# Attention's value product in a two-layer encoder: the values become the stationary operand, two heads share the array

## The chip, the cores and the metric

The kernel runs on one core of a Trainium2 chip. A core has five engines that run their own instruction streams in order and wait for one another through semaphores: TensorE (PE in the profile; its weight loads are listed apart as PEld), VectorE (DVE), ScalarE (ACT), GpSimd (POOL) and SyncE (SP, which here only issues DMAs). The metric is the time of one execution on the device, in microseconds.

## The reference, cut to what matters

Two layers of a streaming encoder on 512 tokens of 1024 features. Each layer: half a SwiGLU block, a mixing block, half a SwiGLU block, a norm. The mixing block has two head groups side by side, attention with 8 heads and a convolution module, whose outputs are concatenated and projected:

```python
for l in range(DEPTH):
    x = x + 0.5 * swiglu(rms_norm(x, ...), ...)
    p = rms_norm(x, mix_norm[l]) @ w_in[l]
    attn = mla_group(p[..., :o_kv], ...)          # 8 heads, 64 value columns each
    conv = conv_group(p[..., o_cv:], ...)         # GLU, depthwise conv of 31 taps, LayerNorm, silu
    x = x + jnp.concatenate([attn, conv], -1) @ w_out[l]
    x = x + 0.5 * swiglu(rms_norm(x, ...), ...)
    x = rms_norm(x, post_norm[l])
```

Inside attention each block of 128 queries sees the keys up to its own end (with a mask inside the last block):

```python
scores = einsum('bhqd,bhkd->bhqk', qs, ks).astype(float32) * scale
probs  = softmax(where(allowed, scores, -1e30))
out    = einsum('bhqk,bhkd->bqhd', probs, vs)
```

All arithmetic is float32 in the reference.

## The kernel before, in words

The residual x is held with features on the 128 partitions and the 512 tokens along the free dimension. The big products use three matmuls of split operands (`mm3`, L154 to L156, a rounded high part and a low remainder); attention itself uses plain float32 matmuls.

The mixing block (`mix_body`) first makes the projections, the queries `q`, the keys `kn` and the values `vs` (four tiles of 128 tokens by 8 x 64 columns, L900). Then attention runs head by head through five stages, written as a software pipeline: `ORDER = "t0s1p3v4o5"` names a stage and its lag in steps, and the loop at the end of attention emits in every step each stage for the head that is due.

- `turn` (L811, L816): transposes of queries and keys on TensorE, copied out by ScalarE (L813) and VectorE (L818).
- `scores` (L834, L835): for query block i a matmul over the (i+1) x 128 visible keys, the mask added by a second matmul; VectorE takes the row maximum (L836, result `mx`), ScalarE the exponential (L840), which also leaves the row's sum in `sums`. The score of block 1 (128x256) shares a bank with that of block 0 and comes last.
- `turn_p` (L855): ten transposes of the 128 x 128 blocks of probabilities, keys on the partitions afterwards; three evictions (L858), two by VectorE and one by ScalarE. Key block j keeps the query blocks j to 3 side by side, 512, 384, 256 and 128 columns.
- `values` (L868): for every query block t and key block j up to t one matmul with the turned probabilities stationary (128 columns) and the head's 64 value columns moving: ten a head. Two heads share a bank `po`. After the odd head VectorE takes 1/sum (L873, 8 numbers a partition) and multiplies it in (L875), so that the result has queries on the partitions and 2 x 64 value columns for each block.
- `turn_out` (L886): four transposes bring that to features on partitions, and `split` (L161 by ScalarE, L162 by VectorE) makes the high and low parts which the output projection reads as `at`.

Beside attention the convolution's taps run: channel groups 0 and 3 on VectorE (L922, one operation a tap, accumulated in PSUM, then copied out by ScalarE, L932), groups 1 and 2 as a product on ScalarE (L926, tile `pr` with three buffers) and an add on GpSimd (L930). Then GpSimd adds the four groups (L944 to L946) and TensorE forms the mean over channels with a matmul against `onesm` (L948). From it follow the LayerNorm, silu and the conv half of the projection's operand (L954 to L966, `cv`); meanwhile TensorE multiplies the attention half for the first output tiles (`early_groups`, L154 to L156).

```python
for c, kind in enumerate("DAAD"):        # cut: D on VectorE, A on ScalarE and GpSimd
    ...
G.tensor_tensor(ysum, ys[0], ys[1], ALU.add)
G.tensor_tensor(ysum, ysum, ys[2], ALU.add)
(G if YP else V).tensor_tensor(ysum, ysum, ys[3], ALU.add)
pm = bank()
T.matmul(pm, onesm, ysum, start=True, stop=True)
```

The order of the instructions on each engine is not that of the source. A planner (`schedule_with_timeline_sim=True`) chooses it from its own costs when the program is built, within the data's dependences and a few `issue_after` bounds. Tiles come from rotating pools: `tmps` (five buffers of 128 x 512), `small`, `ring` (35 buffers), and seven PSUM banks. A tile waits until the one that had its buffer before is no longer read.

Of the kernel before, what the change touches and what calls it, by code (L numbers as in the profile page):

```python
# [7 lines left out]
FP = mybir.dt.float32  # L8
# [4 lines left out]
ALU = mybir.AluOpType  # L13
AX = mybir.AxisListType

P = 128
# [4 lines left out]
NT = S // P  # L21
# [4 lines left out]
DV = 64  # L26
# [48 lines left out]
def encoder_kernel(ctx: ExitStack, tc: tile.TileContext, xT, consts, vecs, rgain, wgu1, wd1, wdq1,  # L75
# [7 lines left out]
    small = ctx.enter_context(tc.tile_pool(name="small", bufs=2))  # L83
# [3 lines left out]
    def nm(s):  # L87
        uid[0] += 1
        return f"{s}{uid[0]}"
# [4 lines left out]
    def tmp(w=S, dt=FP):  # L94
        return tmps.tile([P, w], dt, tag="t", name=nm("t"))

    def bank():
        return psum.tile([P, S], FP, tag="ps", name=nm("ps"))
# [4 lines left out]
    V, A, G, T = nc.vector, nc.scalar, nc.gpsimd, nc.tensor  # L103
# [8 lines left out]
    ident = cst[:, CID:CID + P]  # L112
# [46 lines left out]
    def split(src, made=slot):  # L159
        hi, lo = made(FR), made(FR)  # L160
        order["high"] = A.copy(hi, src).ins  # L161
        order["evicted"] = V.tensor_tensor(lo, src, hi.bitcast(FP), ALU.subtract).ins  # L162
        return hi, lo
# [46 lines left out]
    def spread(r):  # L210

        dg = tmp()
        V.tensor_tensor(dg.rearrange("p (t j) -> p t j", t=NT),
                        ident[:, None, :].to_broadcast([P, NT, P]),
                        r[:, :, None].to_broadcast([P, NT, P]), ALU.mult)
        ps = bank()
        order["spread"] = T.matmul(ps, ones, dg, start=True, stop=True).ins
        return ps
# [398 lines left out]
    def mix_body(kpool, l, gx, norm, done):  # L617
# [28 lines left out]
        cqT, ckT, pq, scqs, vs = [], [], [], [], []  # L646
# [114 lines left out]
        def up_kv(w, t, n=S):  # L761

            ts_ = slice(t * P, (t + 1) * P)
            ps = bank()
            for k in range(2):
                cs = slice(k * n, (k + 1) * n)
                mm3(ps, ckT[k][0][:, ts_], ckT[k][1][:, ts_], w[0][:, cs], w[1][:, cs], k == 0, k == 1)
            return ps
# [33 lines left out]
        at = []  # L802
# [3 lines left out]
        heads = [{} for _ in range(H)]  # L806
# [54 lines left out]
        def values(h):  # L861

            if h % 2 == 0:
                heads[h]["po"] = bank()
            po = heads[h - h % 2]["po"].rearrange("p (t h d) -> p t h d", t=NT, h=2)
            for t in range(NT):
                for j in range(t + 1):
                    T.matmul(po[:, t, h % 2], heads[h]["pt"][j][:, (t - j) * P:(t - j + 1) * P],  # L868
                             vs[j][:, h * DV:(h + 1) * DV], start=j == 0, stop=j == t)
            if h % 2 == 0:  # L870
                return
            rs = small.tile([P, NT, 2], FP, tag="rs", name=nm("rs"))
            V.reciprocal(rs, heads[h - 1]["sums"])  # L873
            o = tmp()
            V.tensor_tensor(o.rearrange("p (t h d) -> p t h d", t=NT, h=2), po,  # L875
                            rs[:, :, :, None].to_broadcast([P, NT, 2, DV]), ALU.mult)
            heads[h]["o"] = o

        def turn_out(h):

            if h % 2 == 0:
                return
            o = heads[h]["o"]
            ps = bank()
            for t in range(NT):
                T.transpose(ps[:, t * P:(t + 1) * P], o[:, t * P:(t + 1) * P], ident)  # L886
            at.append(split(ps, kept if len(at) < 2 else slot))

        STAGES = [({"t": turn, "s": scores, "p": turn_p, "v": values, "o": turn_out}[c], int(d)) for c, d in zip(ORDER[::2], ORDER[1::2])]

        wv = load_w(wkv[l, 1], WC, "uk")
# [4 lines left out]
        with tc.issue_after(order["turned"]):  # L896
            for t in range(NT):
                ps = up_kv(wv, t)
# [5 lines left out]
        for step in range(H + 6):  # L904
            for stage, lag in STAGES:
                h = step - lag
# [7 lines left out]
        for c in range(4):  # L914
# [4 lines left out]
            for k in range(CK - 2, -1, -1):  # L919
# [4 lines left out]
                pr = kpool.tile([P, S], FP, tag="pr", name=nm("pr"), bufs=3)  # L924
# [31 lines left out]
        r = st.token(CW)  # L956
        early_groups(range(E2, E3))
        pr = spread(r)
# [282 lines left out]
```

## Time and profile before

| | us |
|---|---|
| median of 3 runs | 1804.17 (1803.3 to 1804.97) |
| the profiled execution | 1804.94 |
| its span, first to last instruction | 1803.1 |
| PE busy | 1781.6 |
| DVE busy | 1493.0 |
| ACT busy | 1091.9 |
| POOL busy | 420.2 |
| mean granted TensorE clock | 0.998 |

A timeline row gives the start and the time it took in microseconds, engine, line, operation, output<-inputs with shapes and a count; in brackets stands how long the engine sat idle before it and what ended that. Rows that merge several instructions (x4) give the time from the first start to the last end. A table of windows gives, for each stretch, its length and the busy time and number of instructions of PE, PEld, DVE, ACT and POOL, then the granted TensorE clock, the DMA share and GB/s. A group row gives the busy time in all, the mean ns of one, and the idle time before. TensorE's matmuls overlap, so the cost of one in a row of many is the distance between starts, not its own duration. A float32 matmul shows as two records, a transpose as one.

### The profile page before, as it was taken

Reading aid. Unit: us, or ns where it says so; the run is one execution under the profiler, and the core shown is the slowest. Engines: PE = TensorE matmul, PEld = TensorE weight load, DVE = VectorE, ACT = ScalarE, POOL = GpSimd, SP = SyncE. Lnnn points to the kernel's source line nnn. Section 1 sums busy time; section 2 is a strip of 40 time slices with the busy share of each in tenths; the row PEclk is TensorE's granted clock in tenths of the full one; section 3 lists DMA queues with packets and bytes.
Section 4 is the critical chain, followed back from the end, with each engine's and each line's share of the span. In section 5 each row is a group of like instructions: output and inputs, shape, how many; then the busy total and the mean of one; then the engine's idle time right before and its main releaser. Section 6 shows DMA issues by size and latency. Waiting matters only on the chain. (4 is left out here: it accounts for less than half of the span.)

```text
span 1803.1 us, 29267 instructions
## 1 busy us (share of the span) xinstructions
PE 1781.6 (99%) x11334; PEld 1603.1 (89%) x11334; DVE 1493.0 (83%) x2263; ACT 1091.9 (61%) x1721; POOL 420.2 (23%) x343
## 2 busy tenths in 40 slices
PE   9999999999999999999999999999999999999998
PEld 7899999888788899999888999998978788999997
DVE  7898988689956989898779989876998668989884
ACT  5565656457953575756645656554779435656564
POOL 1000010258943000000310000002689410000102
PEclk9999999999999999999999999999999999999999
DMA  5657574325103466665426575743250125575742
GB/s 167 173 127 182 134 174 125 108 88 136 29 24 100 124 167 160 153 159 129 125 63 169 126 191 122 193 110 111 80 151 3 42 83 161 139 183 134 180 119 74
DMA packets 70412, 226.16 MB, mean 125 GB/s; under 512 B 7936, under 2 KB 8320, under 8 KB 70272
## 3 DMA queue, kind: packets, MB, share of 16 engines
q1 hardware_dynamic: 54000, 169.74, 29.7%
q0 software_dynamic: 16128, 54.53, 17.6%
q8 instruction: 89, 1.46, 0.3%
q14 instruction: 51, 0.42, 0.1%
q10 hardware_dynamic: 144, 0.00, 0.0%
HBM read 222.15 MB, written 2.10 MB: 124 GB/s over the span
## 5 line engine op out<-in xcount | busy, mean ns | idle before, releaser
L155 PE MATMUL ps<-r,wh 128*128 128x256 f32 (+1 forms) x2540 | 805.8, 318 | 0.0
L154 PE MATMUL ps<-r,wh 128*128 128x256 f32 (+1 forms) x2540 | 802.9, 320 | 2.3 <-ACT wh L1060 1.5
L156 PE MATMUL ps<-r,wl 128*128 128x256 f32 (+1 forms) x2348 | 750.0, 321 | 1.7 <-DVE wl L246 1.6
L154 PEld LDWEIGHTS ps<-r,wh 128*128 128x128 f32 x2540 | 480.4, 189 | 44.1 <-ACT wh L138 3.7
L155 PEld LDWEIGHTS ps<-r,wh 128*128 128x128 f32 x2540 | 481.4, 190 | 34.2 <-issue 1.4
L156 PEld LDWEIGHTS ps<-r,wl 128*128 128x128 f32 x2348 | 445.0, 190 | 36.7 <-DVE wl L246 3.2
L373 PE MATMUL ps<-xj,wh 128*128 128x512 f32 x864 | 304.8, 392 | 4.6 <-DVE t L426 4.6
L138 ACT CAST wh<-raw 128x1024 fp32r<-128x1024 f32 (+3 forms) x148 | 132.3, 903 | 203.6 <-PE ps L155 100.3
L390 POOL DMA_DIRECT2D ls<-in_wgu x72 | 62.5, 869 | 734.4 <-ACT ls L389 656.5
L244 ACT CAST wh<-fr 128x1024 fp32r<-128x1024 f32 (+1 forms) x160 | 157.8, 986 | 109.7 <-DVE fr L410 51.3
L144 DVE TENSOR_TENSOR wl<-raw,wh 128x1024 fp32r<-128x1024 f32 (+3 forms) x132 | 145.2, 1108 | 84.7 <-ACT wh L138 84.3
L246 DVE TENSOR_TENSOR wl<-fr,wh 128x1024 fp32r<-128x1024 f32 (+1 forms) x160 | 182.1, 1138 | 20.5 <-ACT wh L244 20.5
L373 PEld LDWEIGHTS ps<-xj,wh 128*128 128x128 f32 x864 | 161.3, 188 | 36.3 <-DVE t L426 6.2
L930 POOL TENSOR_TENSOR y<-y,pr 128x511 f32<-128x511 f32 (+14 forms) x120 | 158.1, 1318 | 54.9 <-ACT pr L926 47.5
L374 PE MATMUL ps<-xj,ls 128*128 128x256 f32 x576 | 161.3, 280 | 0.0
L246 DVE TENSOR_TENSOR wl<-raw,wh 128x1024 fp32r<-128x1024 f32 (+1 forms) x100 | 113.4, 1134 | 14.8 <-ACT wh L244 14.4
L244 ACT CAST wh<-raw 128x1024 fp32r<-128x1024 f32 (+1 forms) x100 | 98.1, 981 | 44.7 <-PE ps L155 27.7
L191 POOL TENSOR_TENSOR r<-r,t 128x512 f32<-128x512 f32 x45 | 75.1, 1678 | 175.7 <-ACT t L187 174.9
L374 PEld LDWEIGHTS ps<-xj,ls 128*128 128x128 f32 x576 | 108.3, 188 | 0.2
L389 ACT ACTIVATE ls<-fr 128x1024 fp32r<-128x1024 f32 (+1 forms) x56 | 56.1, 1001 | 85.3 <-PE ps L374 49.5
L926 ACT ACTIVATE pr<-m,vec 128x511 f32<-128x511 f32 (+14 forms) x120 | 85.8, 737 | 12.4 <-POOL y L930 12.4
L922 DVE SCALAR_TENSOR_TENSOR cv<-m,vec,cv 128x511 f32<-128x511 f32 (+14 forms) x120 | 87.8, 732 | 3.6 <-ACT cv L918 2.2
(242 smaller groups left out, 2926.2 us busy)
## 6 DMA issues: line engine op xcount, KB each, us to landing
fr<-in_wgu SPq DMA_DIRECT2D x112, 512.0 KB, 4.2
ls<-in_wgu POOLq DMA_DIRECT2D x72, 512.0 KB, 6.6
raw<-in_wgu SPq DMA_DIRECT2D x62, 512.0 KB, 4.9
fr<-in_wdq SPq DMA_DIRECT2D x48, 384.0 KB, 5.3
ls<-in_wdq POOLq DMA_DIRECT2D x32, 384.0 KB, 4.7
raw<-in_wd SPq DMA_DIRECT2D x32, 384.0 KB, 3.1
raw<-in_wd SPq DMA_DIRECT2D x32, 256.0 KB, 2.7
raw<-in_wcv SPq DMA_DIRECT2D x16, 512.0 KB, 3.6
```

The lines of the kernel that those rows point to most:

```text
L138: order["cast"] = A.copy(hi[:, :w], raw[:, :w]).ins
L144: (G if kind in POOLW.split() else V).tensor_tensor(lo[:, :w], raw[:, :w], hi[:, :w].bitcast(FP), ALU.subtract)
L154: T.matmul(o, lh, rh, start=first, stop=False, skip_group_check=free)
L155: T.matmul(o, lh, rl, start=False, stop=False, skip_group_check=free)
L156: order["mm"] = T.matmul(o, ll, rh, start=False, stop=last, skip_group_check=free).ins
L244: A.copy(hi[:, :w], src[:, :w])
L246: order["lo"] = V.tensor_tensor(lo[:, :w], src[:, :w], hi[:, :w].bitcast(FP), ALU.subtract).ins
L373: T.matmul(o, w[0][:, c], both, start=start and k == 0, stop=False, skip_group_check=True)
L374: last = T.matmul(o[:, 0:HS], w[1][:, c], both[:, 0:HS], start=False, stop=k == 3, skip_group_check=True).ins
L922: V.scalar_tensor_tensor(acc[:, s:], u[c][:, :S - s], tap(k), acc[:, s:], ALU.mult, ALU.add)
L926: A.activation(pr[:, s:], u[c][:, :S - s], AF.Copy, scale=tap(k))
L930: order["conv"] = G.tensor_tensor(acc[:, s:], acc[:, s:], pr[:, s:], ALU.add).ins
```

## The change

The product of probabilities and values is turned round. The values are now stationary (128 keys by 64 columns) and the turned probabilities move, key block by key block, over all query blocks that see them: four matmuls a head with 512, 384, 256 and 128 columns instead of ten with 64. The result has value columns on the partitions and queries along the free dimension: the even head of a pair is written to partitions 0 to 63 of the bank, the odd head to 64 to 127, so each matmul uses one half of the array's columns. Both heads are done when the odd head is due.

As the result no longer needs turning, `turn_out` only splits it. The reciprocal of the sums has queries on the partitions and must be turned instead: VectorE writes it 64 times over, 2 x 64 columns for each of the four query blocks (128 x 512 in all), TensorE turns four blocks, ScalarE copies them out of PSUM, and VectorE multiplies. Lines from L900 on stand one lower in the changed file; the text keeps the numbers of before for what both have, and the new lines are L866 (reciprocal), L870 (its turns), L872 (copy), L876 (matmuls) and L879 (product).

```diff
         def values(h):
             if h % 2 == 0:
-                heads[h]["po"] = bank()
-            po = heads[h - h % 2]["po"].rearrange("p (t h d) -> p t h d", t=NT, h=2)
+                return
+            rs = tmp()
+            V.reciprocal(rs.rearrange("p (t h d) -> p t h d", t=NT, h=2),
+                         heads[h - 1]["sums"][:, :, :, None].to_broadcast([P, NT, 2, DV]))
+            pr = bank()
             for t in range(NT):
-                for j in range(t + 1):
-                    T.matmul(po[:, t, h % 2], heads[h]["pt"][j][:, (t - j) * P:(t - j + 1) * P],
-                             vs[j][:, h * DV:(h + 1) * DV], start=j == 0, stop=j == t)
+                T.transpose(pr[:, t * P:(t + 1) * P], rs[:, t * P:(t + 1) * P], ident)
+            r = tmp()
+            A.copy(r, pr)
+            po = bank()
+            for j in range(NT):
+                for i in range(2):
+                    T.matmul(po[i * DV:(i + 1) * DV, j * P:], vs[j][:, (h - 1 + i) * DV:(h + i) * DV],
+                             heads[h - 1 + i]["pt"][j], start=j == 0, stop=j == NT - 1)
+            o = tmp()
+            V.tensor_tensor(o, po, r, ALU.mult)
+            heads[h]["o"] = o
+
+        def turn_out(h):
             if h % 2 == 0:
                 return
-            rs = small.tile([P, NT, 2], FP, tag="rs", name=nm("rs"))
-            V.reciprocal(rs, heads[h - 1]["sums"])
-            o = tmp()
-            V.tensor_tensor(o.rearrange("p (t h d) -> p t h d", t=NT, h=2), po,
-                            rs[:, :, :, None].to_broadcast([P, NT, 2, DV]), ALU.mult)
-            heads[h]["o"] = o
-
-        def turn_out(h):
-            if h % 2 == 0:
-                return
-            o = heads[h]["o"]
-            ps = bank()
-            for t in range(NT):
-                T.transpose(ps[:, t * P:(t + 1) * P], o[:, t * P:(t + 1) * P], ident)
-            at.append(split(ps, kept if len(at) < 2 else slot))
+            at.append(split(heads[h]["o"], kept if len(at) < 2 else slot))
```

## The prediction

> **What bounds the kernel now.** I read the page's busy line, then a table of windows around the only code that changes (attention, once per layer), then the timeline of that stretch engine by engine.
>
> ```profile
> span 1803.1 us, 29267 instructions
> PE 1781.6 (99%) x11334; PEld 1603.1 (89%) x11334; DVE 1493.0 (83%) x2263; ACT 1091.9 (61%) x1721; POOL 420.2 (23%) x343
> ```
> ```profile
> core 0: us, PE busy (x) PEld busy (x) DVE busy (x) ACT busy (x) POOL busy (x), PEclk, DMA share, GB/s
> 451.00:508.50 57.50, 55.06 (x402) 44.97 (x401) 50.05 (x97) 50.54 (x122) 52.09 (x43) 1.00 0.11 23
> 1344.00:1400.00 56.00, 53.79 (x393) 43.92 (x391) 49.16 (x96) 50.17 (x122) 51.48 (x43) 1.00 0.10 20
> ```
> TensorE looks like the bound overall, but in attention four engines are each within 13% of full: 57.5 us hold 55.1 of PE and 50 to 52 of the other three. What any of them is given there has little room. How the stretch ends:
>
> ```profile
> 493.36 0.72 DVE L922 SCALAR_TENSOR_TENSOR cv<-m,vec,cv 128x483 f32<-128x483 f32 x1
> 493.98 1.15 DVE L836 TENSOR_REDUCE mx<-ps 128x1 f32<-128x384 f32 x2
> 495.05 0.72 DVE L922 SCALAR_TENSOR_TENSOR cv<-m,vec,cv 128x482 f32<-128x482 f32 x1
> 497.59 0.60 ACT L932 COPY m<-cv 128x512 f32<-128x512 f32 x1
> ...
> 463.28 3.96 POOL L930 TENSOR_TENSOR y<-y,pr 128x511 f32<-128x511 f32 x3 [0.61 <-ACT pr L926]
> 467.90 3.95 POOL L930 TENSOR_TENSOR y<-y,pr 128x508 f32<-128x508 f32 x3 [0.67 <-ACT pr L926]
> 472.23 31.42 POOL L930 TENSOR_TENSOR y<-y,pr 128x505 f32<-128x505 f32 x24 [0.37 <-ACT pr L926]
> 503.60 1.27 POOL L944 TENSOR_TENSOR t<-m,y 128x512 f32<-128x512 f32 x1
> ...
> 506.29 1.26 POOL L946 TENSOR_TENSOR t<-t,m 128x512 f32<-128x512 f32 x1
> 507.24 0.69 DVE L875 TENSOR_TENSOR t<-ps,rs 128x512 f32<-128x512 f32 x1 [0.87 <-PE ps L868]
> 507.99 0.66 PE L886 MATMUL ps<-cst,t 128*128 128x128 f32 x4 [0.79 <-DVE t L875]
> 508.48 1.02 PE L948 MATMUL ps<-t,onesm 128*128 128x512 f32 x2
> ...
> 522.52 1.19 PE L154 MATMUL ps<-r,wh 128*128 128x512 f32 x4
> ```
> L948 (the mean over the conv channels) needs POOL's sum L944 to L946, whose last addend is VectorE's conv channel (tap 128x482, then the copy L932). In layer 0 that sum ends at 507.55, the attention tail at 508.4: both arrive together. From L948 a chain leads to 522.52, where the output projection first reads the conv half. So the price of this change is how far L948's start moves, per layer. The second layer has the same shape 892 us later, with one difference:
>
> ```profile
> 1387.06 0.71 DVE L922 SCALAR_TENSOR_TENSOR cv<-m,vec,cv 128x482 f32<-128x482 f32 x1
> 1400.97 2.08 PE L948 MATMUL ps<-t,onesm 128*128 128x512 f32 x2 [0.31 <-POOL t L946]
> 1416.68 1.21 PE L154 MATMUL ps<-r,wh 128*128 128x512 f32 x4
> ```
> ```profile
> 506.77:510.18 3.41, 2.63 (x14) 1.88 (x14) 1.57 (x3) 1.48 (x2) 0.79 (x1) 1.00 0.00 0
> 1397.64:1401.05 3.41, 2.31 (x20) 1.94 (x18) 1.38 (x2) 0.38 (x2) 3.12 (x3) 0.98 0.00 0
> 1401.05:1404.47 3.41, 3.41 (x7) 2.06 (x8) 2.07 (x4) 2.37 (x5) 0.00 (x0) 0.52 0.00 0
> ```
> After 3.41 us in which PE was busy 68%, the granted clock was 0.52 for the next 3.41; after one of 77% it stayed 1.00. L948 to L154 takes 14.04 us in layer 0 and 15.71 in layer 1, so one slow window costs 1.67.
>
> **The change, part by part (layer 0's clock).**
>
> *Matmuls.* Start to start:
>
> ```profile
> 468.27 2.44 PE L868 MATMUL ps<-m,r 128*128 128x64 f32 x20
> 470.55 0.65 PE L834 MATMUL ps<-r,r 96*128 96x256 f32 x2
> ...
> 460.47 1.12 PE L834 MATMUL ps<-r,r 96*128 96x512 f32 x2
> 461.43 0.19 PE L835 MATMUL ps<-mneg,mrow 128*128 128x64 bf16 x1
> ...
> 464.62 0.39 PE L834 MATMUL ps<-r,r 96*128 96x128 f32 x2
> 464.85 0.19 PE L835 MATMUL ps<-mneg,mrow 128*128 128x64 bf16 x1
> 464.88 0.91 PE L834 MATMUL ps<-r,r 96*128 96x384 f32 x2
> 465.62 0.19 PE L835 MATMUL ps<-mneg,mrow 128*128 128x64 bf16 x1
> ...
> 467.14 1.29 PE L855 MATMUL ps<-cst,r 128*128 128x128 f32 x10
> ```
> Removed: 2.28 a head, 4.56 a pair. Added: two heads times moving widths 512, 384, 256, 128; L834 gives 0.96, 0.74, about 0.48 and 0.23, so 2.4 a head: 4.8 a pair one after the other, 2.4 if the halves run together. Before shows no matmul on half the columns; bounds are thus -2.2 and +0.2 a pair, and I take the gain. It matters little, since PE will wait (below). The Trainium skill (TensorEngine Tiling, "Key Properties") says two things that pull apart: tiles run in parallel, and changing the tiling mode drains TensorE, which the changed program does ten times a layer; no row here shows either.
>
> *Turns.* Four L886 turns a pair become four of the reciprocals (new L870): same shape, 0.66 in the row above, no difference; the split reads SBUF instead of PSUM, none either. ScalarE gains a 128x512 copy a pair (L872), 0.61 by the ACT row below, 2.5 a layer: it has 7 us free, so nothing; uncovered, 2.5. Each pair now takes three `tmps` buffers of five instead of one, and the rotation gives POOL's first sum (L944) the buffer of pair 2's turned reciprocals: it has to wait for pair 2's product on VectorE, 506 to 508 in the walk below, where it ran at 503.6. Two adds later, at 509 to 511, POOL is still ahead of the last addend, so this costs nothing here. No DMA moves; SP's and POOL's order is unchanged.
>
> *The reciprocal.* This is the step that decides. L873 took the reciprocal of 8 numbers a partition; the new L866 takes the same 8 broadcast to 512 columns, four times a layer.
>
> ```profile
> L873 DVE RECIPROCAL rs<-sums x8: 187/193/197, 465.0 to 1392.6; 128x8 f32<-128x8 f32 x8
> ```
> ```profile
> L858 DVE COPY r<-ps 128x512 f32<-128x512 f32 x8 | 5.5, 684 | 0.4 <-PE ps L855 0.4
> L858 ACT COPY r<-ps 128x512 f32<-128x512 f32 x8 | 4.9, 614 | 0.8 <-PE ps L855 0.8
> L858 DVE COPY r<-ps 128x256 f32<-128x256 f32 x8 | 3.3, 415 | 0.4 <-PE ps L855 0.4
> ```
> ```profile
> L120 DVE MEMSET minus_half<- 128x8 f32 x1 | 0.1, 65 | 0.0
> ```
> COPY, the other one-input operation, has two sizes: (684-415)/256 = 1.05 ns a column, fixed part 146 ns. Eight columns at that rate would take 154, the reciprocal takes 193. With COPY's fixed part it costs (193-146)/8 = 5.9 ns a column, and 512 columns 3.15 us. Lower bound: any 128x512 operation's 0.69. Upper: MEMSET's fixed part (65-8 = 57), 17 ns a column, 8.8 us. I take 3.15, nearest in kind.
>
> VectorE's lane up to tap 482: 50.05 of work less the last L875 (0.69), plus 4 x (3.15-0.19) = 11.8, makes 61.2: from 451, 512.2 with no idle at all. The changed program's order gives the same from the other end. Head 7's three reductions, at 495.1 before, now come after three reciprocals (+8.9) and ahead of six taps (-3.7; a tap is 0.62 from start to start): near 500. Behind them stand pair 1's split, five evictions, the last reduction and five taps (505.4), pair 2's product (TensorE has it at 505 to 507), the last reciprocal (509 to 511), head 7's evictions, pair 2's split and two taps: 511.9 to 513.9. Then L932's copy (0.60), POOL's last add (1.26) and hand-overs (0.2): L948 starts at 514 to 516 instead of 508.48, +5.5 to +7.5; I take 6.3. Head 7's weights wait for the same evictions, so pair 3's product ends near 512 to 514.5, beside POOL's sum. Layer 1 the same (tap 482 to L948 is 13.9 us there, 13.4 here): 12.6 together.
>
> *Clock.* From 496 to 514 PE has the last score, head 6's and 7's turns, two of reciprocals and two products, some 8 us or 45%, under the 68% that slowed it: layer 0 now pays 1.67 after L948; layer 1 already did.
>
> Sum: 12.6 + 1.7 = 14.3. The profiled execution took 1804.94 (span 1803.1 plus 1.8 around) and becomes 1819.2; the median of the runs is 0.8 lower, so **1818.5**.
>
> **Rivals.**
>
> *The reciprocal has a shorter fixed part than COPY.* At 126 ns, between MEMSET's and COPY's, it costs 8.4 ns a column and 4.4 us: the lane ends at 517.2, L948 at 519.3, +10.8 a layer, 1804.2 + 21.6 + 1.7 = 1827.5. For it: nothing in the rows fixes that part. The Trainium skill (VectorE: DVE Perf Modes, "First, the fixed hardware budget") tells of an iterative divide with a repeat count of 8, by which 512 columns would take 8 x 512 = 4096 cycles; 193 ns for 8 columns is compatible with this if the rest is 126 ns.
>
> *The reciprocal is as cheap as its neighbours (0.69), still slower.* ScalarE then sets the tail. In the changed order all conv products L926 stand ahead of head 7's exponentials, and they have three buffers which POOL frees.
>
> ```profile
> 493.32 0.70 ACT L926 ACTIVATE pr<-m,vec 128x487 f32<-128x487 f32 x1 [0.60 <-POOL y L930]
> ...
> 494.37 0.36 ACT L840 ACTIVATE r<-ps,mx 128x128 f32<-128x128 f32 x1
> ```
> The last product can start three adds (31.42/24 = 1.31 each) before POOL's last add ends: 503.6 - 0.4 - 3.9 = 499.3; head 7's exponentials follow at 500.1, not 494.37. PE's rest from there (last score 0.5, half of head 6's turns and all of head 7's 1.8, two of the reciprocals' 0.9, two products of 2.4 to 4.8, 1.5 for copies between) takes 9.5 to 14: L948 at 509.6 to 514, +1.1 to +5.6; POOL's sum, behind pair 2's product at 505.6 to 508, comes at 509.7 to 512. With 2.6 a layer and the slow window: 1811.
>
> *Faster.* PE ran almost alone from 498 to 508; two pairs' products at half price leave it 4 us less, and pair 3 needs no turn behind its product. L948 is then held by POOL's sum, 507.55 less the waits POOL had (0.61, 0.67, 0.37), at best 505.9. A gain of at most 2.6 a layer, and 1.7 if layer 1 loses its slow window: 1797. It needs a reciprocal under 1.7 us (four of them must add less than the 6.0 us between the lane and L948), halves running together, and head 7 not held by ScalarE. The 0.193 row speaks against the first, the order against the last.
>
> *No change.* The same with PE's gain only filling waits: 1804, within 0.2% (3.6 us, about what a measurement of this kernel can tell from no change).
>
> **Chances.** Reciprocal near 3.15 us, 1818.5 (own range 1811 to 1824): 0.50. The 4.4 us one, 1827.5: 0.22. The cheap one with ScalarE's tail, 1811: 0.16, of which 0.04 lies within 0.2%. No change: 0.06. Faster: 0.06. So faster 0.06, same 0.10, slower 0.84. Below 1806 lie the faster case, no change and the best of the cheap one (0.14), above 1832 the dear end of the reciprocal's bounds (0.06): the range is 1806 to 1832.
>
> **What would show it.** RECIPROCAL 128x512 near 3.2 us, 0.7 or 4.4; VectorE busy without a gap up to tap 482, near 512 to 514; L948 starting at 514 to 516 and waiting for POOL, and POOL's last add for L932; PE with idle gaps from 496 on, and a clock near 0.5 around L948 in layer 0; new matmul pairs starting together or 0.48 apart per pass. The prediction is wrong if the reciprocal is cheap, if the scores that wait behind it starve ScalarE and so POOL much earlier (then more is lost), or if slow-clock windows spread over the whole stage.

## The result and the profile after

The changed kernel took 1830.63 us (median of 4 runs, 1828.4 to 1832.44) against 1803.74 (1802.81 to 1804.97) for the kernel before on the same chip: a ratio of 1.0148, 95% interval 1.0131 to 1.0166. The sign and the range held; the forecast of 1818.5 was 12.1 us too low.

The busy line of the page after:

```profile
span 1828.9 us, 28902 instructions
PE 1791.6 (98%) x11142; PEld 1585.7 (87%) x11142; DVE 1519.3 (83%) x2263; ACT 1099.6 (60%) x1729; POOL 422.3 (23%) x343
```

VectorE has 26.3 us more to do over the span (1519.3 against 1493.0), which is 8 x (3.34 - 0.19) = 25.2 for the reciprocals and little else; the span grew by 25.8. The summary of the new reciprocal's line (fastest, median and slowest in ns, then the first and the last start):

```profile
L866 DVE RECIPROCAL t<-sums x8: 3342/3342/3344, 465.4 to 1418.6; 128x512 f32<-128x512 f32 x8
```

The timeline of the changed kernel at the end of attention in layer 0 and at the same place in layer 1 (L921, L931, L943 to L945 and L947 are the lines that were L922, L932, L944 to L946 and L948):

```profile
517.63 0.98 PE L870 MATMUL ps<-cst,t 128*128 128x128 f32 x4 [3.42 <-DVE t L866]
518.54 3.66 PE L876 MATMUL ps<-r,m 128*64 128x512 f32 x16
...
519.49 0.72 DVE L921 SCALAR_TENSOR_TENSOR cv<-m,vec,cv 128x482 f32<-128x482 f32 x1
520.24 0.59 ACT L931 COPY m<-cv 128x512 f32<-128x512 f32 x1 [0.96 <-DVE cv L921]
520.97 1.27 POOL L945 TENSOR_TENSOR t<-t,m 128x512 f32<-128x512 f32 x1 [4.07 <-ACT m L931]
522.30 1.12 PE L947 MATMUL ps<-t,onesm 128*128 128x512 f32 x2
522.32 0.69 DVE L879 TENSOR_TENSOR t<-ps,t 128x512 f32<-128x512 f32 x1 [2.11 <-PE ps L876]
...
536.73 1.20 PE L154 MATMUL ps<-r,wh 128*128 128x512 f32 x4
...
1426.78 1.12 PE L947 MATMUL ps<-t,onesm 128*128 128x512 f32 x2
...
1441.31 1.21 PE L154 MATMUL ps<-r,wh 128*128 128x512 f32 x4
```

The chain is the predicted one: the last tap, ScalarE's copy, GpSimd's last add (which waited 4.07 us for it), the mean matmul. TensorE's own lane arrives with it: the last pair's products (518.54, 3.66 us long) end at 522.20. But the tap starts at 519.49 instead of 512, and the mean matmul at 522.30 instead of 508.48: 13.8 us in layer 0 (0.37 of it from ahead of attention). In layer 1 it starts 25.8 us later than before; 14.2 of these are layer 0's shift of the first conv product (536.73 against 522.52), and 1.8 arose between there and layer 1's first scores (1359.39 against 1343.43), so 9.8 are attention's own in layer 1. The work from the mean matmul to the conv product took 14.43 and 14.53, against 14.04 and 15.71.

Windows of the changed kernel show what VectorE did up to the end of that tap, and then the stretches of the clock:

```profile
451.00:520.21 69.21, 58.68 (x295) 36.20 (x295) 62.90 (x97) 53.71 (x126) 51.99 (x42) 0.86 0.10 20
...
472.90:479.75 6.85, 6.83 (x24) 4.65 (x24) 5.30 (x10) 4.81 (x12) 6.46 (x6) 0.53 0.01 2
...
490.00:496.80 6.80, 6.18 (x21) 3.85 (x20) 5.54 (x12) 6.58 (x17) 6.41 (x6) 0.53 0.00 0
...
507.05:510.50 3.45, 3.40 (x13) 1.46 (x13) 3.45 (x8) 2.34 (x7) 0.00 (x0) 0.57 0.00 0
...
517.30:520.70 3.40, 3.07 (x10) 1.38 (x12) 2.91 (x6) 1.04 (x2) 0.00 (x0) 0.57 0.01 2
```

VectorE's lane is 62.9 us of work (0.4 of it because the stage starts later) and 6.3 of idle time; 61.2 and none were predicted. Before, it had 0.89 of idle time up to the same tap:

```profile
451.00:495.77 44.77, 43.11 (x296) 33.31 (x295) 43.88 (x86) 43.75 (x108) 40.93 (x34) 1.00 0.14 28
```

TensorE's clock fell to about half four times inside attention, some 20 us in all; before it never did there. Each of the four windows follows 3.4 us in which TensorE was busy for only 1.88, 2.13, 1.78 and 0.30 us, or 55, 63, 52 and 9%, below the 68% that the prediction's rows show ahead of a slow window. The waits of VectorE (DVE) in this stretch (us in total, times, longest), and the rows of the three in the first line:

```profile
DVE mx L836 <- PE ps L835: 2.5, 3, 1.3
DVE t L879 <- ACT pr L925: 1.7, 2, 1.3
DVE mx L836 <- ACT t L872: 1.1, 1, 1.1
...
475.15 0.56 DVE L836 TENSOR_REDUCE mx<-ps 128x1 f32<-128x384 f32 x1 [0.51 <-PE ps L835]
477.07 0.69 DVE L836 TENSOR_REDUCE mx<-ps 128x1 f32<-128x512 f32 x1 [0.71 <-PE ps L835]
495.23 0.69 DVE L836 TENSOR_REDUCE mx<-ps 128x1 f32<-128x512 f32 x1 [1.26 <-PE ps L835]
```

The second and third row name ScalarE as what came last; the work VectorE reads there (`mx` from scores, `t` from products) comes from TensorE. So it waits for TensorE's scores and products, while TensorE in its turn waits for the reciprocal (3.42 us in the row of L870 above). The slow clock stands between the two: all three waits of the first row fall in the first two slow windows, in which TensorE was busy for 6.83 of 6.85 and 6.18 of 6.80 us, and the wait of 1.1 us ends at 480.77, just behind the first.

### The profile page after: what moved, and what is told of

It is laid out like the page before. It is cut to its first block, busy times and chain, and to the rows that moved or that the text cites. A ratio compares the mean times of both kernels' runs of the same rounds, so it can differ in the third digit from the quotient of the medians.

```text
span 1828.9 us, 28902 instructions
## 1 busy us (share of the span) xinstructions
PE 1791.6 (98%) x11142; PEld 1585.7 (87%) x11142; DVE 1519.3 (83%) x2263; ACT 1099.6 (60%) x1729; POOL 422.3 (23%) x343
## 5 line engine op out<-in xcount | busy, mean ns | idle before, releaser
L921 DVE SCALAR_TENSOR_TENSOR cv<-m,vec,cv 128x511 f32<-128x511 f32 (+14 forms) x120 | 87.6, 730 | 3.8 <-ACT cv L917 2.2
```

The costliest lines, as they stand in the source:

```text
L921: V.scalar_tensor_tensor(acc[:, s:], u[c][:, :S - s], tap(k), acc[:, s:], ALU.mult, ALU.add)
```

## The experiments

Four explanations of the doubled shift were to be told apart: the sum of VectorE's work; the 3.3 us for which one instruction blocks its lane; the slow clock of a TensorE that has less to do; and something in the other parts of the change. Each ratio is to the kernel before on the same chip, with its 95% interval. Attention itself starts up to 1 us earlier or 1.5 later from run to run (GpSimd's add of 128x511, at 463.28 before, shows by how much); where it matters, the shift is given.

**The reciprocal of 8 numbers, and a copy that spreads it** (of the changed kernel):

```diff
-            rs = tmp()
-            V.reciprocal(rs..., sums[..., None].to_broadcast([P, NT, 2, DV]))
+            sm = small.tile([P, NT, 2], FP, tag="rs", name=nm("rs"))
+            V.reciprocal(sm, heads[h - 1]["sums"])
+            rs = tmp()
+            V.tensor_copy(rs..., sm[:, :, :, None].to_broadcast([P, NT, 2, DV]))
```

> The changed kernel, but the reciprocal is taken of the 8 sums (0.19 us) and a plain copy writes it 64 times over (128x512, 0.69): 2.46 us less on VectorE, four times a layer, 9.8 a layer. Theory 1, the long reciprocal in VectorE's in-order lane is the whole cause: the mean matmul comes back from 522 to 509 to 511 in layer 0, and the time to 1804 to 1811. Theory 2, the emptier TensorE falls into slow-clock windows of its own accord and these hold the stage: at least three windows near 0.5 stay in layer 0's attention, and of the 26 us only about 12 come back: 1815 to 1822.

1814.69 us, ratio 1.005 (1.0035 to 1.0065). 15.9 of the 26.9 us came back, and the mean matmul starts at 511.31, of whose 2.83 us of shift 1.28 come from ahead of the stage: in layer 0 attention is only 1.55 us longer than before. The time lies between the forecasts, so the long reciprocal is not the whole cause, but theory 2's slow windows are absent: the mean clock of attention is 0.98, and VectorE is full up to its last tap.

```profile
451.00:501.87 50.87, 45.85 (x281) 29.82 (x279) 50.79 (x96) 50.66 (x123) 45.79 (x37) 1.00 0.15 32
...
451.00:523.00 72.00, 61.88 (x357) 41.62 (x356) 61.84 (x113) 58.30 (x135) 55.82 (x44) 0.98 0.10 23
...
511.31 1.13 PE L948 MATMUL ps<-t,onesm 128*128 128x512 f32 x2 [3.89 <-POOL t L946]
```

TensorE has the same matmuls as in the changed kernel, yet keeps its clock: without the long reciprocal the slow windows of this stage are gone. What is still lost lies behind the mean matmul of layer 0 (15.69 us to the conv product, with a slow window, against 14.04) and in layer 1, whose attention is 4.0 us longer than before.

**No wide operation on VectorE for it at all:**

```diff
-            V.reciprocal(rs..., ...)        # cut: the long one goes, and its buffer with it
+            V.reciprocal(sm, heads[h - 1]["sums"])
             for t in range(NT):
-                T.transpose(pr[:, t * P:(t + 1) * P], rs[:, t * P:(t + 1) * P], ident)
+                for i in range(2):
+                    T.matmul(pr[i * DV:(i + 1) * DV, t * P:(t + 1) * P],
+                             sm[:, t, i:i + 1].to_broadcast([P, DV]), ident, start=True, stop=True)
```

> The changed kernel, but nothing 128x512 wide is left to VectorE for the reciprocal: 8 numbers (0.19), and the turn is a product of the 64-fold repeated column of weights with the identity, eight of 64x128 a pair instead of four turns. VectorE has 12.6 us less a layer than in the changed kernel, TensorE some 1 to 1.3 more. Theory 1: the mean matmul at 506 to 510, 1799 to 1806. Theory 2: slow windows stay, some 1812 to 1820.

1812.81 us, ratio 1.0041 (1.0027 to 1.0054). Theory 1's 1799 to 1806 fails: with the reciprocal as cheap as before the change, the rest of it still loses 8.5 us. Now the mean matmul waits for GpSimd (POOL); a slow window follows that wait.

```profile
507.09 0.86 DVE L162 TENSOR_TENSOR r<-t,r 128x512 fp32r<-128x512 f32 x1 [0.69 <-ACT r L161]
...
507.48 1.59 POOL L944 TENSOR_TENSOR t<-t,y 128x512 f32<-128x512 f32 x1
509.14 1.26 POOL L945 TENSOR_TENSOR t<-t,m 128x512 f32<-128x512 f32 x1
...
510.46 2.08 PE L947 MATMUL ps<-t,onesm 128*128 128x512 f32 x2 [4.87 <-POOL t L945]
...
507.00:510.40 3.40, 0.00 (x0) 0.00 (x0) 0.86 (x1) 1.34 (x2) 3.24 (x3) 0.79 0.00 0
510.50:517.30 6.80, 6.80 (x17) 4.72 (x18) 4.47 (x7) 2.60 (x5) 0.00 (x0) 0.61 0.00 0
```

An add that took 1.26 on GpSimd took 1.59 beside the split L162, which in the changed kernel reads two operands from SBUF. The cost shows on both sides (line summary: fastest, median and slowest in ns, and group rows of the adds, before and then here):

```profile
L162 DVE TENSOR_TENSOR r<-ps,r x2: 692/692/692, 505.7 to 509.3; 128x512 fp32r<-128x512 f32 x2
...
L930 POOL TENSOR_TENSOR y<-y,pr 128x487 f32<-128x487 f32 (+29 forms) x36 | 44.8, 1244 | 4.2 <-ACT pr L926 1.6
```
```profile
L162 DVE TENSOR_TENSOR r<-t,r x2: 859/1120/1382, 503.7 to 507.1; 128x512 fp32r<-128x512 f32 x2
...
L929 POOL TENSOR_TENSOR y<-y,pr 128x487 f32<-128x487 f32 (+29 forms) x36 | 46.0, 1279 | 5.0 <-ACT pr L925 2.6
```

**The kernel before with the long reciprocal alone:**

```diff
-            rs = small.tile([P, NT, 2], FP, tag="rs", name=nm("rs"))
-            V.reciprocal(rs, heads[h - 1]["sums"])
+            rs = tmp()
+            rs4 = rs.rearrange("p (t h d) -> p t h d", t=NT, h=2)
+            V.reciprocal(rs4, heads[h - 1]["sums"][:, :, :, None].to_broadcast([P, NT, 2, DV]))
             ...                             # cut: the product reads rs4 as it is
```

> The kernel before with one edit: its reciprocal (8 numbers) is taken 64 times over, 128x512, as in the changed kernel; the old products, turns and splits stay. VectorE has 12.6 us more a layer. Theory 1: the mean matmul moves by 10 to 14 a layer, as in the changed kernel, and the time is 1824 to 1832. Theory 2: TensorE has 2.2 us a pair more to do than in the changed kernel, slow windows are fewer, and the lane alone decides: the mean matmul moves by 5 to 8, 1814 to 1820.

1833.75 us, ratio 1.0158 (1.0142 to 1.0173): theory 1. This one edit costs as much as the whole change (the intervals overlap). It has the old products and turns, so neither the halves of the array nor TensorE's saved work is needed for the loss. 25.2 us of added VectorE work cost about 29. Here it is the attention tail behind the last reciprocal, not the tap, that ends last. Up to the end of the last product VectorE idled 4.5 us, and the clock of that stretch was 0.95, where it was 0.86 in the changed kernel:

```profile
512.50 3.34 DVE L874 RECIPROCAL t<-sums 128x512 f32<-128x512 f32 x1
...
518.93 0.69 DVE L876 TENSOR_TENSOR t<-ps,t 128x512 f32<-128x512 f32 x1 [1.62 <-PE ps L868]
...
520.59 1.92 PE L949 MATMUL ps<-t,onesm 128*128 128x512 f32 x2
...
451.00:519.62 68.62, 60.76 (x404) 48.46 (x402) 64.13 (x99) 53.19 (x125) 52.84 (x43) 0.95 0.11 23
```

**The pair's products twice** (of the changed kernel):

```diff
+            for again in range(2):
                 for j in range(NT):
                     for i in range(2):
                         T.matmul(po[...], vs[j][...], heads[h - 1 + i]["pt"][j], ...)
```

> The changed kernel, but each pair's eight products of values and probabilities are done twice into the same bank (the second time from zero, so nothing is left out): TensorE has about 2.3 us more a pair, as much as before the change. Theory 1: nothing is gained, the pair's product only comes 2.3 us later: 1830 to 1840. Theory 2: the fuller TensorE keeps its clock, of four slow windows in layer 0 two or more go, and with them at least 5 us: 1815 to 1825.

1843.27 us, ratio 1.0201 (1.0178 to 1.0224). More work for TensorE made it slower by 12.6 us, beyond even theory 1's 1840. Each product stands behind a reciprocal's turns or evictions and ahead of VectorE's next step, so its 2.3 us seem to be paid for in part (12.6 of 8 x 2.3 = 18.4; this reading is not tested). Theory 2's condition was hardly met: over 451 to 523 the clock was 0.89, against 0.86 in the changed kernel.

**The reciprocal a head at a time** (of the changed kernel): two of half the width, at two places.

```diff
             if h % 2 == 0:
-                return
-            rs = tmp()
-            V.reciprocal(rs..., heads[h - 1]["sums"][:, :, :, None].to_broadcast([P, NT, 2, DV]))
+                heads[h]["rs"] = tmp()
+            rs = heads[h - h % 2]["rs"]
+            V.reciprocal(rs...[:, :, h % 2], heads[h - h % 2]["sums"][:, :, h % 2, None].to_broadcast(...))
+            if h % 2 == 0:
+                return
```

> The changed kernel, with the reciprocal taken a head at a time: two of 128x256 (by the two ends, (3343-193)/504 = 6.25 ns a column, 1.74 us each) instead of one of 128x512. The work on VectorE is the same to 0.15 us a pair, the longest single stop in its lane is half. Theory sum (what counts is VectorE's work up to the last tap): 1829 to 1833. Theory block (what counts is that one 3.3 us instruction starves the other engines behind it, which then starve VectorE): the 6.3 us of VectorE's idle time per layer go by half or more, 1818 to 1826.

1831.23 us, ratio 1.0148 (1.0127 to 1.0169), the same as the changed kernel, as theory sum has it. But the run tells less than it was meant to: the planner parted the two halves only for the first pair and put them back to back for the other three, so the block stayed as long there.

```profile
461.82 1.74 DVE L866 RECIPROCAL t<-sums 128x256 f32<-128x256 f32 x1
465.00 1.74 DVE L866 RECIPROCAL t<-sums 128x256 f32<-128x256 f32 x1
481.66 3.36 DVE L866 RECIPROCAL t<-sums 128x256 f32<-128x256 f32 x2
500.67 3.35 DVE L866 RECIPROCAL t<-sums 128x256 f32<-128x256 f32 x2
513.33 3.35 DVE L866 RECIPROCAL t<-sums 128x256 f32<-128x256 f32 x2
...
451.00:519.41 68.41, 57.65 (x295) 35.79 (x295) 63.46 (x100) 53.20 (x125) 51.61 (x42) 0.86 0.09 19
```

VectorE still idles 4.95 us. Whether four reciprocals in short pieces with other work between them would lose less stays open.

**Filler for TensorE while it waits for the reciprocal** (of the changed kernel):

```diff
             pr = bank()
+            for _ in range(10):
+                T.matmul(pr[:, 0:P], ones, ones, start=True, stop=True)
```

> The changed kernel, with ten idle products of ones (128x128, about 0.22 us each) into the bank of the turned reciprocals ahead of their turns, so that TensorE is busy there while it waits for the long reciprocal; the result is overwritten, nothing is left out. Theory clock: the slow windows in attention (20.5 us in layer 0, 13.7 in layer 1) go by half or more and with them VectorE's waits for scores: 1820 to 1827. Theory lane: VectorE's 12.6 us of added work a layer sets the end whatever the clock: 1828 to 1834.

1836.18 us, ratio 1.0181 (1.0166 to 1.0196). The time rose, beyond even theory lane's 1834, although the clock of the stage in layer 0 rose too, from 0.86 to 0.91. This does not refute theory clock, because the filler did not do what it was meant to: two slow stretches of 6.8 us stayed in layer 0 (from 471.4 and from 491.8, both at 0.51), 13.6 of 20.5 us. And it takes time of TensorE itself: VectorE's waits moved to the products, which now stood behind the filler (6.1 us against 1.7). The windows of the changed kernel, then of this one, and its largest wait:

```profile
451.00:523.00 72.00, 61.37 (x310) 37.56 (x308) 63.59 (x98) 54.30 (x127) 53.26 (x43) 0.86 0.09 19
```
```profile
451.00:523.00 72.00, 64.20 (x377) 43.91 (x376) 61.84 (x96) 53.83 (x125) 52.43 (x43) 0.91 0.08 17
...
DVE t L881 <- PE ps L878: 6.1, 2, 4.2
```

**The product written back into PSUM** (of the run without a wide operation), so that the split reads PSUM again:

```diff
-            o = tmp()
+            o = po
             V.tensor_tensor(o, po, r, ALU.mult)
```

> The run without a wide reciprocal (1812.8), with one more edit: the product of values and turned reciprocals is written back into its PSUM bank, so that the split reads PSUM again as before the change, and a pair takes one temporary buffer fewer. Theory port: GpSimd's adds took 1.364 us on average there against 1.309 before, the long ones (1.59) beside the split that reads two SBUF operands; with the split on PSUM no add takes 1.59, GpSimd's sum ends 1.3 us earlier a layer, 1809 to 1811. Theory ScalarE: GpSimd is held by the later products of ScalarE alone, and the time stays at 1812 to 1814.

1808.88 us, ratio 1.0026 (1.0016 to 1.0037): theory port. The adds are back at 1245 ns, L944 at 1.26, the split at 0.69, and the mean matmul starts at 507.50. That is a microsecond earlier than before the change, but attention starts 0.96 earlier too (GpSimd's add of 128x511 at 462.32 against 463.28), so it is level; against the run without a wide operation the stretch from that add (128x509 in layer 1) to the mean matmul is 1.6 us shorter in layer 0 and 1.4 in layer 1, about the 1.3 that was expected. GpSimd waited for no temporary buffer in either run, so the freed buffer is not what did it.

```profile
L929 POOL TENSOR_TENSOR y<-y,pr 128x487 f32<-128x487 f32 (+29 forms) x36 | 44.8, 1245 | 5.0 <-ACT pr L925 2.6
...
507.50 2.07 PE L947 MATMUL ps<-t,onesm 128*128 128x512 f32 x2 [4.23 <-POOL t L945]
...
524.07 1.20 PE L154 MATMUL ps<-r,wh 128*128 128x512 f32 x4
```

And yet it loses 5 us. Half of that is seen in layer 0: from the mean matmul to the conv product it now takes 16.57 us instead of 14.04. TensorE, done with attention early, idled 4.23 us for GpSimd and then ran at a granted clock of 0.50 for the next 3.4 us.

**The channel sum in another order**, on the run above and on the kernel before:

```diff
-        G.tensor_tensor(ysum, ys[0], ys[1], ALU.add)
-        G.tensor_tensor(ysum, ysum, ys[2], ALU.add)
-        (G if YP else V).tensor_tensor(ysum, ysum, ys[3], ALU.add)
+        V.tensor_tensor(ysum, ys[0], ys[3], ALU.add)
+        G.tensor_tensor(ysum, ysum, ys[1], ALU.add)
+        V.tensor_tensor(ysum, ysum, ys[2], ALU.add)
```

> The run with the product in PSUM, and the sum over the conv channels in another order: VectorE adds groups 0 and 3, GpSimd group 1, VectorE group 2, so that one add of 0.7 us follows GpSimd's last add in place of three of 1.27. If GpSimd's lane is what sets the mean matmul without the long reciprocal: 3 us a layer earlier, 1803 to 1806. If TensorE's and ScalarE's tail of attention sets it: within 1 us of the run with the product in PSUM.

> The kernel before with the new order of the channel sum alone. GpSimd's sum and the attention tail end together there (507.55 and 508.4), so the tail takes over: 0 to 1.5 us a layer, 1801 to 1804.

On the changed form 1804.8 us, ratio 1.0001 (0.999 to 1.0012): level with before, as GpSimd's lane was indeed what held the mean matmul (506.10 in layer 0). The stretch from the start of attention to the mean matmul became 1.6 us shorter in each layer, half of the 3 us expected. On the kernel before, a miss: 1811.92, ratio 1.0041 (1.0027 to 1.0054), 8 us slower. There the planner put VectorE's first sum behind the last pair's work, and GpSimd waited for it:

```profile
507.69 0.68 DVE L944 TENSOR_TENSOR t<-m,m 128x512 f32<-128x512 f32 x1
508.46 1.27 POOL L945 TENSOR_TENSOR t<-t,y 128x512 f32<-128x512 f32 x1 [5.15 <-DVE t L944]
...
510.60 1.22 PE L948 MATMUL ps<-t,onesm 128*128 128x512 f32 x2 [2.11 <-DVE t L946]
```

**TensorE's gap ahead of the mean matmul filled with real work.** `E1 = 1` puts one early output group ahead of the mean matmul, on the run with the new sum and on the kernel before; `WOG = 4` then adds a fourth group to the former.

```diff
-E1 = 0
+E1 = 1
```
```diff
-WOG = 3
+WOG = 4
```

> The run with the channel sum on VectorE (1804.8, equal to before), with one number changed (E1 from 0 to 1): the first of the three early output groups stands ahead of the mean matmul in TensorE's order instead of behind it. There TensorE idled for 2.64 and 3.98 us before the mean matmul and then ran 3.4 to 6.8 us at half clock. Theory idle: the group's nine ready products (0.235 each, 2.1 us) fill the gap, the slow window after the mean matmul in layer 0 goes, mean matmul to first conv product falls from 15.65 and 16.57 to 14 or less: 1798 to 1802. Theory latency: what follows the mean matmul is set by the LayerNorm's chain, TensorE only idles later there: 1803 to 1806.

> The kernel before with the same one number changed (E1 from 0 to 1), as the control for the run with the group in the gap. TensorE has no gap there before the change (0.79 us), so the group only delays the mean matmul or waits beside it: 1804 to 1809.

> The run with the group in the gap (1804.2), with four early output groups instead of three (WOG from 3 to 4), so that TensorE has one more group (twelve products of 0.235, 2.8 us) before the conv half is ready. There it idled 1.89 us before the sums of the LayerNorm (L198) in layer 0. Theory TensorE: it fills that gap and has 2.8 us less behind it, 1 to 2 us a layer: 1800 to 1803. Theory chain: the LayerNorm's chain from the mean matmul to the conv half (13.5 to 14 us without a slow window) sets the end, and the group stands in its way: 1804 to 1808.

1804.18 (ratio 1.0001, 0.9992 to 1.0009), 1810.54 (1.0037, 1.0023 to 1.0052) and 1803.4 (1.0001, 0.9992 to 1.001). On the changed form theory latency holds: the mean matmul moved back behind the group, to 508.04 in layer 0, and TensorE found its gap later on, 1.89 us ahead of L198. Only layer 1 lost its slow window (13.50 to the conv product). The kernel before got slower by 6 us, a little more than expected. The fourth group changed nothing that can be measured, so its two theories stay undecided. No version beat the kernel before.

## Why the prediction was right in sign and short in size

- *What decides.* Right: the wide reciprocal is the step. Put into the kernel before it alone costs 29.4 us; taken out of the changed one it gives 16 to 18 back. The size is another matter: the time lies outside the favoured case's own 1811 to 1824. That it lies inside 1806 to 1832 is luck, since the range reached that far only for a dearer reciprocal, which did not come.
- *The reciprocal, 3.15 us.* Nearly right: 3.34. The two ends give (3342-193)/504 = 6.25 ns a column where 5.9 was taken. The rival at 4.4 us is refuted by this row, which shows three quarters of that; its 1827.5 came nearer to the result for a wrong reason. The Trainium skill (VectorE: DVE Perf Modes, "First, the fixed hardware budget") names a repeat count of 8 for the reciprocal. Read as eight passes a column, at the 8.4 ns that the rival took for them, this would be an estimate of 4.3 us for 512 columns; the row does not agree with that reading.
- *VectorE's lane, "512.2 with no idle at all".* This is the step that failed. The tap ended at 520.2: 1.7 us more work than summed, of which 4 x 0.19 = 0.8 is the reciprocal's price and 0.4 the stage's later start, and 6.3 us of idle time that the sum had set to zero without a reason. So 6.3 of shift a layer became 13.4 and 9.8, 10.6 us more in all than the 12.6 of the forecast. Some 3 us more arose outside attention, 1.8 of them ahead of layer 1's, and no run explains them. Before, VectorE found its operands ready (0.89 us idle); with the reciprocal in the lane the two wait for each other in turn, TensorE for the reciprocal and VectorE for the scores and products. The long reciprocal in the old kernel makes VectorE idle too, 4.5 us in layer 0, without the rest of the change. That the idle time is this mutual wait is read from the waits, and was not switched off by itself. How much of it hangs on the slow clock that follows TensorE's own waits is open: the loss with the long reciprocal in the old kernel was as large at a higher clock (0.95 against 0.86 in layer 0), but in the changed kernel layer 0, with some 20 us of slow windows in attention, lost 13.4 us, and layer 1, with some 13.5, lost 9.8 at nearly the same work of VectorE (62.5 and 61.8 us). How much hangs on the 3.3 us coming in one piece is open as well, as the pieces of the run by heads mostly stayed together.
- *Clock, +1.67 after the mean matmul in layer 0.* Wrong place. That stretch took 14.43 and 14.53: 0.4 more in layer 0, 1.2 less in layer 1. The slow windows came inside attention instead, four in layer 0, as the last lines of the prediction had feared. They go along with the loss, and the run with the short reciprocal shows that they come with the long one; how much they add is open, as said above. Where TensorE idles just ahead of the mean matmul the stretch behind it is up to 2.5 us longer (16.57 against 14.04).
- *Matmuls, 2.4 a pair if the halves run together.* Right: 2.31 from the first record to the next work, where 4.8 was the price one after the other:

```profile
480.59 2.38 PE L876 MATMUL ps<-r,m 128*64 128x512 f32 x16
482.90 0.64 PE L811 MATMUL ps<-cst,q 128*96 128x128 f32 x4
```

  That agrees with the first of the two things which the Trainium skill says of tiles (TensorEngine Tiling, "Key Properties"), that they work in parallel. The cost of switching the mode was not measured by itself.
- *"The split reads SBUF instead of PSUM", no difference.* Wrong, and hidden by the larger error. VectorE's split and GpSimd's adds held each other up, 0.69 against up to 1.38 us and 1.26 against 1.59. The Trainium skill has the rule (SBUF — State Buffer, "Who interferes with whom"): a VectorE instruction with two SBUF inputs contends with a GpSimd instruction that reads SBUF. The run with the product in PSUM agrees: it makes the stage 1.6 and 1.4 us shorter in the two layers, some 3 of the 3.9 us between the two runs' times.
- *The rotation of temporary buffers makes L944 wait, at no cost.* Right: GpSimd's first sum waited 7.43 us for the product L879, and its last add then still waited 4.07 for the tap.
- *"PE ran almost alone from 498 to 508", under "Faster".* Misread: in these 10 us of the kernel before GpSimd was busy for 9.09, TensorE for 9.21. Once the reciprocal is cheap, the mean matmul waits for GpSimd's lane, by 3.89, 4.87 and 4.23 us in the runs shown.
- *The rival of a cheap reciprocal, 1811.* The runs without it gave 1812.8 and 1814.7, but not by ScalarE's tail: GpSimd's lane, lengthened by the split, and then a slow window made the loss. The right size came from another mechanism.

## What to carry to other kernels

When work is added to a lane that runs beside others at nearly 90%, take its sum as the lower end of the price: here idle time of half the added work came on top (6.3 us on 12.6), so put the idle time that may appear into the forecast, not only into its conditions. Broadcast after a costly operation, not before it: eight reciprocals and a copy take 0.9 us where 512 take 3.34. When an operand moves from PSUM to SBUF, look at who else reads SBUF at that time.

## What the hardware showed unexpectedly

- RECIPROCAL on VectorE costs 6.25 ns a column, six times a copy's 1.05.
- VectorE's subtraction of two SBUF operands and GpSimd's adds hold each other up, to 1.38 us from 0.69 and to 1.59 from 1.26; in the changed kernel one add beside such a subtraction took 1.98.
- Where TensorE had nothing to do for 3.4 us (0.00 busy from 507.00 to 510.40, in the run without a wide operation), the granted clock was 0.79 there and only 0.61 over the next 6.8, in which it was fully busy: the slow time falls on the work behind the gap.
